# Weighted key-value recurrence on one core: logs, inverses and outputs in three successive slots, all even loads on GpSimd

## The chip, the cores and the metric

One core of a Trainium2 chip runs the program. The metric is the device time of the whole execution in microseconds. TensorE is PE, VectorE is DVE, ScalarE is ACT, GpSimd is POOL and SyncE is SP.

## The reference

For 16 sequences of 2048 steps and 256 channels, a decaying weighted mean of v with weights exp(k) is kept, in a form that is safe against overflow (pp is the running maximum):

```python
for t in range(seq_len):
    ww = u + kk
    qq = np.maximum(pp, ww)
    e1 = np.exp(pp - qq)
    e2 = np.exp(ww - qq)
    output[b, t, :] = (e1 * aa + e2 * vv) / (e1 * bb + e2 + 1e-08)
    ww = pp - w + kk
    qq = np.maximum(ww, kk)
    e1 = np.exp(ww - qq)
    e2 = np.exp(kk - qq)
    aa = e1 * aa + e2 * vv
    bb = e1 * bb + e2
    pp = qq
```

Here kk and vv are k and v at one time. aa, bb and pp are carried along the time, each with 256 channels, for each sequence by itself.

## The kernel before, in words

**Tiles.** Time lies on the partitions. The 2048 times are a head of 32 and 16 steps of TC = 126, each step two halves of 63. A pair is four sequences at one step: a tile `kr` and a tile `vr` of 126 x 4 x 256 numbers. So a step has four pairs, and with two pairs for the head there are NP = 66, numbered n. For each pair PE multiplies k by two triangular matrices (`logs`, L287, into `X`), ACT takes the exponential of the result (`exps`, L301 for the first eight pairs and L303 later, into `ez`), and DVE multiplies it by v (`times_v`, L319). `round_k` (L271, `km`) and `cast_v` (L311, `vb`) are DVE's casts ahead of these.

**State.** `sums` (L349) adds each half's totals of a step over the partitions into one bank, `tot`. After a step's last pair, at slot s, these totals are copied (`copy_sums`, L358), turned by PE (`turn_sums`, L365), split (`split_sums`, L372), and carried on by small DVE and ACT operations: a log (`lf`), offsets (`S`), a clamp (`near`), weights (`w`, `g`), the state itself (`tb`, `da`, `AB`), a log and an exponential for scaling (`y`, `phi`), a product (`ab`). PE turns the result (L455), DVE copies it to `row` (L460), and SyncE's transfers (L464, `inject`) write it as rows 126 and 127 of `ez` of the same step's pairs. With these rows in place the matmuls of `den` and `num` give the outputs of that step, the carried state included.

**Outputs.** Ten slots after its exponentials (six for the head) a pair's denominator is summed by PE (`den`, L488), ACT takes its log and exp(-log) (`recip`, L499 and L500), PE sums the numerator (`num`, L509, one half of the pair at a time), DVE multiplies (`mult`, L517) and the result is stored (`store`, L535).

**Slots and order.** The main loop's turn n is slot n. In it `exps(n)`, `recip(q)` for the pair q whose output is due, `num`, `mult` and `store` of the pair due one slot earlier, and `logs(n + 1)` are recorded; the order in which they are recorded is the order on each engine, since the helper `K` chains the instructions of an engine. After slot 65 only outputs are left. Small state operations stand at named places of the slot (`small_work`), by a table of slots after s.

**Buffers and banks.** Four `kr` and four `vr` tiles, so loads run four slots ahead; two `km` and two `vb`; seven `ez` tiles of two pairs each; five result tiles `rd`. Of the eight PSUM banks X takes four, den two (one tile), num one and tot one until slot 66; den's and num's tiles serve the two turns as well. After slot 65 den has two tiles and num three.

**Queues.** SP issues the v loads, the first k loads and the state rows; POOL issues the k loads (L128) and the stores. Both execute their lists in order.

Of the kernel before, what the change touches and what calls it, by code (L numbers as in the profile page):

```python
# [7 lines left out]
F32 = mybir.dt.float32  # L8
# [14 lines left out]
def kernel(  # L23
# [29 lines left out]
    TC = 2 * HS  # L53
# [54 lines left out]
    def load(n):  # L108
        kr = kpool.tile([128, 4, Dm], F32, tag="kr", name="kr")
        vr = vpool.tile([128, 4, Dm], F32, tag="vr", name="vr")  # L110
        kr_of[n], vr_of[n] = kr, vr
        c, p = pairs[n]
        if is_head(n):
            if p == 1:
                K(POOL.memset(kr[64:96, 0:2, :], 0.0))
                K(POOL.memset(vr[64:96, 0:2, :], 0.0))
            for t, x in ((kr, k), (vr, v)):
                for g in range(NG):
                    b = 6 * g + 4 * p
                    e = min(b + 2 * tiles_of(n), B)  # L120
                    if b < e:
                        K(SP.dma_start(out=t[g * GB:(g + 1) * GB, 0:e - b, :],
                                        in_=x[b:e, 0:T0, :].rearrange("n t d -> t n d")))
        else:
            t0 = T0 + c * TC
            r = min(128, T - t0)
            for t, x, eng in ((kr, k, SP if n <= AHEAD else POOL), (vr, v, SP)):
                K(eng.dma_start(  # L128
                    out=t[0:r, :, :], in_=x[4 * p:4 * p + 4, t0:t0 + r, :].rearrange("n t d -> t n d")))


# [252 lines left out]
        K(SC.activation(lf, st[c, "t"][:, 4:6], ACT.Ln))  # L384
        st[c, "lf"] = lf

    def state_offsets(c):
        lf = st.pop((c, "lf"))
        for h in range(2):
            i = 2 * c + h  # L390
            K(DVE.scalar_tensor_tensor(S[:, i + 1], S[:, i], 0.0, lf[:, h], ALU.max, ALU.add))
        near = tiny.tile([128, 3, 32], F32, tag="near", name="near")
        K(DVE.tensor_scalar(near, S[:, 2 * c:2 * c + 3], NEAR, -NEAR, ALU.min, ALU.max))
        st[c, "near"] = near
# [21 lines left out]
        K(DVE.scalar_tensor_tensor(AB[0][:, :, 0], by_two(st.pop((c, "g"))[:, 0]), 1.0, t[:, :, 0],  # L416
                                   ALU.min, ALU.mult))

    def state_step(c, h):
        if h == 0:  # L420
            t = st.pop((c, "t"))[:, 0:4].rearrange("p (q h) x -> p q h x", q=2)
            tb = small.tile([128, 2, 2, 32], F32, tag="tb", name="tb")
            K(DVE.scalar_tensor_tensor(tb, by_two(st.pop((c, "w"))), 1.0, t, ALU.min, ALU.mult))  # L423
            st[c, "tb"] = tb
        cur = AB[c]
        if h == 1:
            AB[c + 1] = small.tile([128, 2, 2, 32], F32, tag="AB", name="AB")
        da = tiny.tile([128, 2, 32], F32, tag=f"da{h}", name=f"da{h}")
        K(DVE.tensor_add(da, cur[:, :, h], st[c, "tb"][:, :, h]))
        K(DVE.scalar_tensor_tensor(cur[:, :, 1] if h == 0 else AB[c + 1][:, :, 0], by_two(st[c, "g"][:, h + 1]), 1.0,  # L430
                                   da, ALU.min, ALU.mult))

    def inject_logs(c):
        y = tiny.tile([128, 2, 32], F32, tag="y", name="y")
# [4 lines left out]
    def inject_weights(c):  # L439
        f = tiny.tile([128, 2, 32], F32, tag="phi", name="phi")  # L440
        K(SC.activation(f, st.pop((c, "y")), ACT.Exp, scale=-1.0, bias=cc[:, 5:6]))
        st[c, "phi"] = f

    def carries(c):

        ab = tiny.tile([128, 4, 2, 16], BF16, tag="ab16", name="ab16")
        f, f2 = st.pop((c, "phi")), tiny.tile([128, 2, 32], F32, tag="phi2", name="phi2")
        K(DVE.scalar_tensor_tensor(f2, st[c, "g"][:, 0:2], 1.0, f, ALU.max, ALU.min))
        K(DVE.tensor_mul(ab, AB[c].rearrange("p q h (j x) -> p (h j) q x", j=2),
                         f2.rearrange("p h (j x) -> p (h j) x", j=2).unsqueeze(2).broadcast_to([128, 4, 2, 16])))  # L450
        st[c, "ab"] = ab

    def turn_carries(c):
        d = bank("num", [128, D]) if wide else bank("den", [128, 2, D])[:, 0]
        K(PE.matmul(d[:, 0:128], st.pop((c, "ab")).rearrange("p m q x -> p (m q x)"), Id, start=True, stop=True))  # L455
        st[c, "d"] = d

    def inject(c):
        row = small.tile([128, 128], BF16, tag="row", name="row")
        K(DVE.tensor_copy(row, st.pop((c, "d"))[:, 0:128]))  # L460
        for j in range(2):
            for h in range(2):
                p = 64 * h + 32 * j
                K(SP.dma_start(out=EZ[group_of(c, j)][TC + h:TC + h + 1, 0:2, :, :].rearrange(  # L464
                                   "o q i (x c) -> o (q i x) c", c=128),
                               in_=row[p:p + 32, :]))

# [19 lines left out]
                            skip_group_check=True))  # L489
        DEN[n] = d  # L490

    def recip(n):
        r = NH if is_head(n) else TC
        i = tiles_of(n)
        rd = rpool.tile([128, 2, D], F32, tag="rd", name="rd")
        d = DEN.pop(n)
        for a in ((0, 1), (1, 2)) if n == NP - 1 else ((0, i),):
            a = slice(*a)
            K(SC.activation(rd[0:r, a, :], d[0:r, a, :], ACT.Ln, scale=RS))  # L499
            K(SC.activation(rd[0:r, a, :], rd[0:r, a, :], ACT.Exp, scale=-1.0))  # L500
        RD[n] = rd

    def num(n, i):
        if i >= tiles_of(n):
# [14 lines left out]
    def store(n):  # L519
# [10 lines left out]
        else:  # L530
            c, p = pairs[n]
            t0 = T0 + c * TC

            for a, b, eng in ((0, 2, POOL), (2, 4, SP)) if n == NP - 1 else ((0, 4, POOL),):
                K(eng.dma_start(out=out[4 * p + a:4 * p + b, t0:t0 + TC, :].rearrange("n t d -> t n d"),  # L535
                                in_=o[0:TC, a:b, :]))


    later = {}
    for c in range(-1, NST):  # L540
        s = last_of[c]
        work = [(s + 1, "sums", copy_sums), (s + 1, "last", turn_sums)]
        first, second = lambda c: state_step(c, 0), lambda c: state_step(c, 1)
        if c < 0:
            work += [(s + 2, "sums", split_sums), (s + 2, "act", state_logs),
                     (s + 3, "exp", state_weights), (s + 3, "pool", state_start)]
        else:
            work += [(s + 1, "last", split_sums), (s + 2, "first" if c else "exp", state_logs),
                     (s + 2, "sums", state_offsets), (s + 2, "sums", state_weights), (s + 2, "pool", first),
                     (s + 2, "act", inject_logs), (s + 3, "exp", inject_weights),  # L550
                     (s + 3, "pool", carries), (s + 3, "last", turn_carries), (s + 3, "last", inject)]
            if c + 1 < NST:
                work.append((s + 4 if c else s + 3, "pool", second))
            else:

                work = [(s + 1, "act", copy_sums), (s + 2, "sums", turn_sums), (s + 2, "sums", split_sums),
                        (s + 3, "first", state_logs), (s + 3, "sums", state_offsets), (s + 3, "act", state_weights),
                        (s + 3, "last", first), (s + 4, "act", inject_logs), (s + 4, "act", inject_weights),
                        (s + 4, "last", carries), (s + 5, "pool", turn_carries), (s + 5, "pool", inject)]
        for slot, where, f in work:  # L560
            later.setdefault((slot, where), []).append((f, c))

    def small_work(n, where):
        for f, c in later.pop((n, where), []):
            f(c)

    for slot, where, f in ((0, "exp", matrices_for_sums), (1, "pool", matrices_for_head),
                           (4, "dve", matrices_for_outputs),
                           (5, "dve", more_matrices_for_outputs)):
        later.setdefault((slot, where), []).append((lambda c, f=f: f(), None))  # L570

    patterns_for_head()
    round_k(0)
# [3 lines left out]
        K(DVE.tensor_copy(t[96:98], row_of(96, 98)))  # L577

    out_at = {n + (LAG - 4 if is_head(n) else LAG): n for n in range(NP)}
    for n in range(NP + LAG + 1):  # L580
        q, qp = out_at.get(n), out_at.get(n - 1)
        live, out_q, out_qp = n < NP, q is not None, qp is not None
        if n == NP:
            widen()
        if n + AHEAD < NP:
            load(n + AHEAD)
        small_work(n, "first")
        if live:
            exps(n)
        elif out_q:  # L590
            den(q)
            recip(q)
        small_work(n, "exp")
        if 0 < n <= NP:
            sums(n - 1)
        if n + 1 < NP:
            round_k(n + 1)
        small_work(n, "sums")
        if out_qp:
            num(qp, 0)  # L600
            if not live:
                num(qp, 1)
        if live and out_q:
            den(q)
            recip(q)
        if out_qp:
            mult(qp, 0)
            if live:
                num(qp, 1)
        small_work(n, "pool")  # L610
        if live:
            times_v(n)
        if out_qp:
            mult(qp, 1)
            store(qp)
        if n + 1 < NP:
            logs(n + 1)
            cast_v(n + 1)
        small_work(n, "dve")
        small_work(n, "act")  # L620
        small_work(n, "last")
    assert not later


# [28 lines left out]
```

## Time and profile before

| what | value |
|---|---|
| median of 5 runs | 334.43 us (330.21 to 335.71) |
| the profiled execution | 335.08 us, its span 333.4 us |
| busy: PE, DVE, ACT, POOL | 86%, 85%, 83%, 34% |
| granted TensorE clock, mean | 0.978 |
| HBM read and written | 68.10 MB and 33.55 MB, 305 GB/s over the span |
| DMA queue of POOL (q0) | 19232 packets, 65.27 MB |
| DMA queue of SP (q1) | 39858 packets, 36.93 MB |
| first and last start of L303 (pairs 8 to 65) | 39.5 and 290.9 us |

The page comes from one execution. A group of instructions has its source line, engine, output and input names, count, busy time, mean duration in ns, and the idle time just before it with what ended it. An arrow to the left reads "waited for". The DMA share is the mean busy share of sixteen DMA engines, summed over the queues.

### The profile page before, as it was taken

How to read it: one execution, taken by the hardware profiler on the slowest of the kernel's cores; microseconds unless marked ns; L12 is line 12 of the kernel's file. 1: busy time of each engine (PE TensorE's matmuls, PEld its weight loads, DVE VectorE, ACT ScalarE, POOL GpSimd, SP SyncE). 2: the span in 40 equal slices, each digit the busy share in tenths (PEclk: the TensorE clock that was granted, in tenths of full speed). 3: DMA queues.
4: the chain of work that ended last, by engine and by line, in shares of the span. 5: the costliest groups of instructions: out<-in, count | busy, mean ns of one | idle time of the engine just before them, and what ended most of it. 6: DMA issues, size and time to landing. Idle time of an engine off the chain costs nothing.

```text
span 333.4 us, 4078 instructions
## 1 busy us (share of the span) xinstructions
PE 286.9 (86%) x1200; PEld 137.3 (41%) x1200; DVE 284.3 (85%) x571; ACT 277.8 (83%) x310; POOL 114.3 (34%) x162
## 2 busy tenths in 40 slices
PE   0696988799999998999999999999998999998480
PEld 0333444344445453545454444444453545443130
DVE  2878798989898999999999989898989999968260
ACT  2647589699999999998999999999999998999370
POOL 6221224504243434425243434243334433122131
PEclk9999799999999999999999999999999999999787
DMA  7999859899999999999999999999999999747545
GB/s 250 240 336 340 285 176 329 248 310 331 326 376 348 374 343 375 328 366 342 377 329 373 349 373 342 346 361 343 373 353 369 311 304 316 237 130 214 161 147 164
DMA packets 59120, 102.47 MB, mean 307 GB/s; under 512 B 7610, under 2 KB 43162, under 8 KB 59098
## 3 DMA queue, kind: packets, MB, share of 16 engines
q0 software_dynamic: 19232, 65.27, 56.0%
q1 hardware_dynamic: 39858, 36.93, 36.3%
q8 instruction: 9, 0.15, 0.2%
q14 instruction: 13, 0.11, 0.1%
q10 hardware_dynamic: 8, 0.00, 0.0%
HBM read 68.10 MB, written 33.55 MB: 305 GB/s over the span
## 4 chain that ended last, share of the span: by engine, by line
PE 47%; DVE 26%; ACT 9%; DMA 7%; issue 7%; SPq 1%; POOL 0%; POOLq 0%; DVEq 0%; ACTq 0%
PE X L287 13%; PE num L509 12%; PE tot L349 11%; PE den L488 6%; DVE ez L319 6%; DVE rd L517 5%; DVE km L271 5%; DMA kr<-in_k_dram 5%; PE den L365 4%; ACT ez L303 4%; DVE vb L311 3%; DVE tsum L372 2%; DMA ez<-row 1%; DVE tb L423 1%; ACT rd L499 1%
## 5 line engine op out<-in xcount | busy, mean ns | idle before, releaser
L535 POOL DMA_DIRECT2D out_dram<-rd x64 | 58.6, 917 | 173.6 <-ACT rd L500 77.0
L303 ACT ACTIVATE ez<-X 128x2048 bf16<-128x2048 f32 x58 | 107.8, 1859 | 4.5 <-PE X L287 4.5
L517 DVE TENSOR_TENSOR rd<-num,rd 126x512 f32<-126x512 f32 (+1 forms) x131 | 88.8, 684 | 12.5 <-issue 7.1
L319 DVE TENSOR_TENSOR ez<-ez,vb 126x2048 bf16<-126x2048 bf16 (+1 forms) x66 | 79.8, 1209 | 2.6 <-ACT ez L301 2.1
L499 ACT ACTIVATE rd<-den 126x1024 f32<-126x1024 f32 (+2 forms) x67 | 67.0, 1000 | 12.3 <-PE den L488 11.7
L500 ACT ACTIVATE rd<-rd 126x1024 f32<-126x1024 f32 (+2 forms) x67 | 69.6, 1038 | 2.1
L287 PE MATMUL X<-km,NLE 128*128 128x512 f32 x128 | 52.7, 494 | 15.2 <-DVE km L271 12.8
L128 POOL DMA_DIRECT2D kr<-in_k_dram x61 | 48.0, 787 | 30.3 <-DVE km L271 11.6
L349 PE MATMUL tot<-ez,OHV 126*48 126x512 bf16 x128 | 50.1, 391 | 8.4 <-DVE ez L319 8.4
L509 PE MATMUL num<-ez,LfN 128*128 128x512 bf16 x128 | 49.8, 389 | 5.6 <-DVE rd L517 5.5
L349 PE MATMUL tot<-ez,OHE 128*48 128x512 bf16 x128 | 51.1, 399 | 0.0
L509 PE MATMUL num<-ez,IdN 126*128 126x512 bf16 (+1 forms) x131 | 50.5, 386 | 0.0
L271 DVE CAST km<-kr 126x1024 fp32r<-126x1024 f32 x64 | 44.6, 698 | 4.8 <-ACT km L205 4.7
L311 DVE CAST vb<-vr 126x1024 bf16<-126x1024 f32 (+1 forms) x66 | 45.2, 685 | 0.0
L488 PE MATMUL den<-ez,Lf 128*128 128x512 bf16 x128 | 39.0, 386 | 5.1 <-DMA ez<-row 4.5
L287 PE MATMUL X<-km,NLZ 128*128 128x512 f32 x128 | 41.1, 403 | 0.0
L488 PE MATMUL den<-ez,Id 126*128 126x512 bf16 (+1 forms) x131 | 40.0, 386 | 0.0
L287 PEld LDWEIGHTS X<-km,NLE 128*128 128x128 f32 x128 | 24.1, 196 | 27.7 <-DVE km L271 9.7
L287 PEld LDWEIGHTS X<-km,NLZ 128*128 128x128 f32 x128 | 24.8, 194 | 6.1 <-ACT ez L301 0.3
L349 PEld LDWEIGHTS <-OHE 128*48 128x48 bf16 x128 | 13.3, 104 | 33.5 <-issue 26.9
L509 PEld LDWEIGHTS <-LfN 128*128 128x128 bf16 x128 | 12.5, 98 | 32.4 <-issue 23.8
L509 PEld LDWEIGHTS <-IdN 126*128 126x128 bf16 (+1 forms) x131 | 12.9, 99 | 23.1 <-issue 21.6
(101 smaller groups left out, 204.9 us busy)
## 6 DMA issues: line engine op xcount, KB each, us to landing
out_dram<-rd POOLq DMA_DIRECT2D x63, 504.0 KB, 7.2
vr<-in_v_dram SPq DMA_DIRECT2D x60, 512.0 KB, 4.9
kr<-in_k_dram POOLq DMA_DIRECT2D x57, 512.0 KB, 8.2
vr<-in_v_dram SPq DMA_DIRECT2D x4, 504.0 KB
kr<-in_k_dram POOLq DMA_DIRECT2D x4, 504.0 KB, 10.7
kr<-in_k_dram SPq DMA_DIRECT2D x3, 512.0 KB, 6.4
ez<-row SPq DMA_DIRECT2D x64, 8.0 KB, 6.9
kr<-in_k_dram SPq DMA_DIRECT2D x3, 128.0 KB
```

The source lines that it names most:

```text
L271: K(DVE.tensor_copy(KM[n][0:r, 0:i, :], kr_of.pop(n)[0:r, 0:i, :]))
L287: K(PE.matmul(X[q][:, i, :], m[0:kr, :], km[0:kr, i, :], start=True, stop=True))
L303: K(SC.activation(ez_of(n)[:, 0:4:2], X[2][:, :, 0:i, :], ACT.Exp))
L311: K(DVE.tensor_copy(vb[0:r, 0:i, :], vr_of.pop(n)[0:r, 0:i, :]))
L319: K(DVE.tensor_mul(ez[0:r, 1:4:2], ez[0:r, 0:4:2], vb[0:r, 0:i, :].unsqueeze(1).broadcast_to([r, 2, i, D])))
L349: K(PE.matmul(TOT[c], m[0:r, :], ez_of(n)[0:r, q, i, :], start=n == first_of[c] and i == 0 and q == 0, stop=n == last_of[c] and i == tiles ...
L488: K(PE.matmul(d[:, i, :], m[0:r, :], ez_of(n)[0:r, q, i, :], start=q == 0, stop=q == 2, skip_group_check=True))
L499: K(SC.activation(rd[0:r, a, :], d[0:r, a, :], ACT.Ln, scale=RS))
L500: K(SC.activation(rd[0:r, a, :], rd[0:r, a, :], ACT.Exp, scale=-1.0))
L509: K(PE.matmul(d, m[0:r, :], ez_of(n)[0:r, q, i, :], start=q == 1, stop=q == 3, skip_group_check=True))
L517: K(DVE.tensor_mul(RD[n][0:r, i, :], NUM.pop((n, i))[0:r, :], RD[n][0:r, i, :]))
L535: K(eng.dma_start(out=out[4 * p + a:4 * p + b, t0:t0 + TC, :].rearrange("n t d -> t n d"), in_=o[0:TC, a:b, :]))
```

## The change

Outputs take three slots instead of two: `log_den` in slot n with `den`, `invert` in slot n + 1 ahead of the next pair's log, `num`, `mult` and `store` in slot n + 2. The loop has one slot more. Within a slot `logs(n + 1)` and `cast_v(n + 1)` now stand ahead of `times_v(n)`, and `sums(n)` follows in the same slot instead of the next. The state operations are single functions placed by plans for the head, the first step, the even steps and the last; in the even steps the state rows are issued in slot s + 5, for the first step in slot s + 4, for the last in s + 4.

From pair 4 on k and v are loaded by POOL (the two head pairs stay on SP). The 64 values of both halves go from `row` to `ez` in two transfers of 64 rows each instead of four of 32. A store is split: 120 partitions by POOL, the last six by SP; both halves of the last pair are split so.

Left out in the diff are the split of the state functions that only rearranges them, the old table of places, and the places of the constant matrices.

```diff
@@ -124,8 +124,8 @@
         else:
             t0 = T0 + c * TC
             r = min(128, T - t0)
-            for t, x, eng in ((kr, k, SP if n <= AHEAD else POOL), (vr, v, SP)):
-                K(eng.dma_start(
+            for t, x in ((kr, k), (vr, v)):
+                K((SP if n < 2 else POOL).dma_start(
                     out=t[0:r, :, :], in_=x[4 * p:4 * p + 4, t0:t0 + r, :].rearrange("n t d -> t n d")))
...
-    def state_offsets(c):
-        lf = st.pop((c, "lf"))
-        for h in range(2):
-            i = 2 * c + h
-            K(DVE.scalar_tensor_tensor(S[:, i + 1], S[:, i], 0.0, lf[:, h], ALU.max, ALU.add))
+    def state_offset(c, h):
+        i = 2 * c + h
+        K(DVE.scalar_tensor_tensor(S[:, i + 1], S[:, i], 0.0, st[c, "lf"][:, h], ALU.max, ALU.add))
+
+    def state_near(c):
         near = tiny.tile([128, 3, 32], F32, tag="near", name="near")
         K(DVE.tensor_scalar(near, S[:, 2 * c:2 * c + 3], NEAR, -NEAR, ALU.min, ALU.max))
         st[c, "near"] = near
...
+    def state_decay(c, h):
         if h == 1:
             AB[c + 1] = small.tile([128, 2, 2, 32], F32, tag="AB", name="AB")
-        da = tiny.tile([128, 2, 32], F32, tag=f"da{h}", name=f"da{h}")
-        K(DVE.tensor_add(da, cur[:, :, h], st[c, "tb"][:, :, h]))
-        K(DVE.scalar_tensor_tensor(cur[:, :, 1] if h == 0 else AB[c + 1][:, :, 0], by_two(st[c, "g"][:, h + 1]), 1.0,
-                                   da, ALU.min, ALU.mult))
+        K(DVE.scalar_tensor_tensor(AB[c][:, :, 1] if h == 0 else AB[c + 1][:, :, 0],
+                                   by_two(st[c, "g"][:, h + 1]), 1.0, st.pop((c, "da")), ALU.min, ALU.mult))
...
     def inject(c):
         row = small.tile([128, 128], BF16, tag="row", name="row")
         K(DVE.tensor_copy(row, st.pop((c, "d"))[:, 0:128]))
         for j in range(2):
-            for h in range(2):
-                p = 64 * h + 32 * j
-                K(SP.dma_start(out=EZ[group_of(c, j)][TC + h:TC + h + 1, 0:2, :, :].rearrange(
-                                   "o q i (x c) -> o (q i x) c", c=128),
-                               in_=row[p:p + 32, :]))
+            K(SP.dma_start(out=EZ[group_of(c, j)][TC:TC + 2, 0:2, :, :].rearrange(
+                               "h q i (x c) -> h (q i x) c", c=128),
+                           in_=row[64 * j:64 * j + 64, :]))
...
-    def recip(n):
+    def log_den(n, a=0, b=None):
         r = NH if is_head(n) else TC
-        i = tiles_of(n)
-        rd = rpool.tile([128, 2, D], F32, tag="rd", name="rd")
-        d = DEN.pop(n)
-        for a in ((0, 1), (1, 2)) if n == NP - 1 else ((0, i),):
-            a = slice(*a)
-            K(SC.activation(rd[0:r, a, :], d[0:r, a, :], ACT.Ln, scale=RS))
-            K(SC.activation(rd[0:r, a, :], rd[0:r, a, :], ACT.Exp, scale=-1.0))
-        RD[n] = rd
+        b = tiles_of(n) if b is None else b
+        if a == 0:
+            RD[n] = rpool.tile([128, 2, D], F32, tag="rd", name="rd")
+        K(SC.activation(RD[n][0:r, a:b, :], DEN[n][0:r, a:b, :], ACT.Ln, scale=RS))
+
+    def invert(n, a=0, b=None):
+        r = NH if is_head(n) else TC
+        b = tiles_of(n) if b is None else b
+        K(SC.activation(RD[n][0:r, a:b, :], RD[n][0:r, a:b, :], ACT.Exp, scale=-1.0))
...
-            for a, b, eng in ((0, 2, POOL), (2, 4, SP)) if n == NP - 1 else ((0, 4, POOL),):
-                K(eng.dma_start(out=out[4 * p + a:4 * p + b, t0:t0 + TC, :].rearrange("n t d -> t n d"),
-                                in_=o[0:TC, a:b, :]))
+            for a, b in ((0, 2), (2, 4)) if n == NP - 1 else ((0, 4),):
+                for r0, r1, eng in ((0, 120, POOL), (120, TC, SP)):
+                    K(eng.dma_start(
+                        out=out[4 * p + a:4 * p + b, t0 + r0:t0 + r1, :].rearrange("n t d -> t n d"),
+                        in_=o[r0:r1, a:b, :]))
...
+    PLANS = {
+        "head": ((1, "a0", copy_sums), (1, "p1", turn_sums), (1, "d5", split_sums), (2, "a1", state_logs),
+                 (3, "a0", state_weights), (3, "d4", state_start)),
+        "first": ((1, "a0", copy_sums), (1, "p1", turn_sums), (1, "d5", split_sums), (2, "a0", state_logs),
+                  (2, "d4", state_offset, 0), (2, "d4", state_offset, 1), (2, "d4", state_near),
+                  (2, "a1", state_weights), (3, "d0", state_sums), (3, "d0", state_add, 0),
+                  (3, "d1", state_decay, 0), (3, "a0", inject_logs), (3, "a1", inject_weights),
+                  (4, "d0", carry_weights), (4, "d0", carries), (4, "p0", turn_carries), (4, "d1", inject),
+                  (4, "d4", state_add, 1), (4, "d5", state_decay, 1)),
+        "steady": ((1, "a0", copy_sums), (1, "p1", turn_sums), (1, "d5", split_sums), (2, "a0", state_logs),
+                   (2, "d4", state_offset, 0), (2, "d5", state_offset, 1), (3, "d0", state_near),
+                   (3, "a0", state_weights), (3, "d4", state_sums), (3, "d5", state_add, 0),
+                   (4, "d0", state_decay, 0), (4, "a0", inject_logs), (4, "a0", inject_weights),
+                   (4, "d5", carry_weights), (5, "d0", carries), (5, "p0", turn_carries), (5, "d1", inject),
+                   (5, "d4", state_add, 1), (5, "d5", state_decay, 1)),
+        "last": ((1, "a0", copy_sums), (1, "p1", turn_sums), (1, "d5", split_sums), (2, "a0", state_logs),
+                 (2, "d2", state_offset, 0), (2, "d2", state_offset, 1), (2, "d2", state_near),
+                 (2, "a1", state_weights), (3, "d0", state_sums), (3, "d0", state_add, 0),
+                 (3, "d0", state_decay, 0), (3, "a1", inject_logs), (3, "a1", inject_weights),
+                 (4, "d0", carry_weights), (4, "d0", carries), (4, "p0", turn_carries), (4, "d1", inject)),
+    }
...
+        for slot, where, f, *args in PLANS["head" if c < 0 else "first" if c == 0 else
+                                           "last" if c + 1 == NST else "steady"]:
+            at(last_of[c] + slot, where, f, c, *args)
...
     out_at = {n + (LAG - 4 if is_head(n) else LAG): n for n in range(NP)}
-    for n in range(NP + LAG + 1):
-        q, qp = out_at.get(n), out_at.get(n - 1)
-        live, out_q, out_qp = n < NP, q is not None, qp is not None
+    for n in range(NP + LAG + 2):
+
+        q, qi, qp = out_at.get(n), out_at.get(n - 1), out_at.get(n - 2)
+        live, more, out_q, out_qi, out_qp = n < NP, n + 1 < NP, q is not None, qi is not None, qp is not None
         if n == NP:
             widen()
         if n + AHEAD < NP:
             load(n + AHEAD)
-        small_work(n, "first")
         if live:
             exps(n)
-        elif out_q:
-            den(q)
-            recip(q)
-        small_work(n, "exp")
-        if 0 < n <= NP:
-            sums(n - 1)
-        if n + 1 < NP:
+        small_work(n, "d0")
+        if more:
             round_k(n + 1)
-        small_work(n, "sums")
         if out_qp:
             num(qp, 0)
             if not live:
                 num(qp, 1)
-        if live and out_q:
+        small_work(n, "p0")
+        small_work(n, "d1")
+        small_work(n, "a0")
+        if out_qi and qi < NP - 1:
+            invert(qi)
+        if out_q:
             den(q)
-            recip(q)
+            if q < NP - 1:
+                log_den(q)
+            else:
+                for i in range(2):
+                    log_den(q, i, i + 1)
+                    invert(q, i, i + 1)
         if out_qp:
             mult(qp, 0)
             if live:
                 num(qp, 1)
-        small_work(n, "pool")
+        small_work(n, "d2")
+        if more:
+            cast_v(n + 1)
+        small_work(n, "d3")
+        if more:
+            logs(n + 1)
         if live:
             times_v(n)
+        small_work(n, "p1")
+        if live:
+            sums(n)
+        small_work(n, "d4")
         if out_qp:
             mult(qp, 1)
             store(qp)
-        if n + 1 < NP:
-            logs(n + 1)
-            cast_v(n + 1)
-        small_work(n, "dve")
-        small_work(n, "act")
-        small_work(n, "last")
+        small_work(n, "d5")
+        small_work(n, "a1")
     assert not later
 
```

## The prediction, made before the changed kernel was run

> **What bounds the kernel now.** I read the page's busy shares first, then the windows, the waits of the even stretch, the timeline of one step, and last the end of the run. Four pairs of images make one time step; slot n is one turn of the main loop.
>
> ```profile
> PE 286.9 (86%) x1200; PEld 137.3 (41%) x1200; DVE 284.3 (85%) x571; ACT 277.8 (83%) x310; POOL 114.3 (34%) x162
> ...
> L303 ACT ACTIVATE ez<-X 128x2048 bf16<-128x2048 f32 x58 | 107.8, 1859 | 4.5 <-PE X L287 4.5
> L517 DVE TENSOR_TENSOR rd<-num,rd 126x512 f32<-126x512 f32 (+1 forms) x131 | 88.8, 684 | 12.5 <-issue 7.1
> L319 DVE TENSOR_TENSOR ez<-ez,vb 126x2048 bf16<-126x2048 bf16 (+1 forms) x66 | 79.8, 1209 | 2.6 <-ACT ez L301 2.1
> L499 ACT ACTIVATE rd<-den 126x1024 f32<-126x1024 f32 (+2 forms) x67 | 67.0, 1000 | 12.3 <-PE den L488 11.7
> L500 ACT ACTIVATE rd<-rd 126x1024 f32<-126x1024 f32 (+2 forms) x67 | 69.6, 1038 | 2.1
> ```
>
> Three engines are equally full. The windows show that the even stretch is fuller still, and the end is not:
>
> ```profile
> 200.00:220.00 20.00, 19.07 (x84) 9.45 (x83) 19.01 (x37) 18.80 (x21) 7.28 (x9) 1.00 1.03 346
> 310.00:320.00 10.00, 7.04 (x19) 2.56 (x20) 2.20 (x4) 3.77 (x4) 1.59 (x2) 0.66 0.41 123
> ```
>
> Columns are PE, PEld, DVE, ACT, POOL busy, clock, DMA share, GB/s. At 95% on three engines no single one is the limit: they wait for each other. The waits between 100 and 280 us, ten steps:
>
> ```profile
> ACT lf L384 <- DVE tsum L372: 6.8, 10, 0.7
> PE tot L349 <- DVE ez L319: 5.6, 10, 0.6
> DVE tb L423 <- ACT w L403: 3.8, 10, 0.4
> PE num L509 <- DVE rd L517: 3.5, 20, 0.2
> ACT rd L499 <- PE den L488: 3.4, 10, 0.6
> ```
>
> Each is a state operation, or a log, standing one slot too close to what it needs; no load is waited for. The big exponentials time the slots:
>
> ```profile
> 60.77 1.88 ACT L303 ACTIVATE ez<-X 128x2048 bf16<-128x2048 f32 x1 [1.74 <-PE X L287]
> ...
> 290.88 1.86 ACT L303 ACTIVATE ez<-X 128x2048 bf16<-128x2048 f32 x1
> ```
>
> These are pairs 13 and 65: 230.1 us / 52 = 4.425 us a slot, 17.70 a step. At the end:
>
> ```profile
> 307.28 3.74 SPq L464 DMA_DIRECT2D ez<-row  x4
> 312.96 1.01 PE L488 MATMUL den<-ez,Lf 128*128 128x512 bf16 x2 [4.48 <-DMA ez<-row]
> 314.87 1.02 ACT L499 ACTIVATE rd<-den 126x1024 f32<-126x1024 f32 x1 [5.03 <-PE den L488]
> ```
>
> The last step's state rows cost a stop of 4.5 us, after which PE runs at half rate (den's second pair begins 0.81 us after the first instead of 0.43) until 319.
>
> **The Trainium skill.** DMA: Bandwidth & Descriptors, "Why a DMA increments its semaphore by 16 and not by 1": a SyncE transfer uses the largest number of engines up to 16 that divides the slowest dimension of both sides. By this the old row transfers (32 rows on both sides) used 16 engines, the new (destination 2 x 32 x 128) use 2; no run here shows it yet. Same page, "SWDGE vs HWDGE vs iDMA": the DMA engine alternates between queues at packet boundaries. The trace agrees on packet size: q0 carries 65.27 MB in 19232 packets, q1 36.93 in 39858. SBUF — State Buffer, "Who interferes with whom": two-port copies on VectorE can lock GpSimd out of writing descriptors; here a load's issue takes 0.77 us beside a busy VectorE, which includes it.
>
> **The even stretch, step by step.** Start-to-start times from the timeline around 150 us. ACT: exponential 1.75 (152.75 to 154.50), inverse 0.97; log 1.05 if its inverse follows, estimated 0.92 if not. DVE: cast or product 0.60, product with v 1.13. PE: first num 0.44, den 0.88, second num to X 0.25, X 1.21, sums 0.99: 3.77 a slot, and 1.02 + 0.16 a step for the two turns: 16.26. Small ACT and DVE operations as their rows say, less 0.08 overlap. A crossing to another engine costs 0.05.
>
> Now each slot's PE order is num, den, num, X, sums; ACT exponential, inverse of the slot before, log; DVE km, product, vb, product with v, product. Plain slot: num0 ends 0.60, product 0.65 to 1.33, second num 1.38, X 1.63 to 2.91, product with v 1.85 to 3.07, sums' second matmul 3.12, slot ends 3.87. ACT has 0.2 to spare. With the state work (s is a step's last slot):
> - s+1 = s+5: state product and km on DVE, then the row copy ends at 1.04 and den starts at 1.09 instead of 0.44; X 2.22; the turn of the sums waits for the log, which now stands behind copy and inverse and ends at 3.31: no wait, 3.35 to 4.38; sums end at 5.37.
> - s+2: offsets go after the product with v, hidden: 3.87.
> - s+3: clamp before km moves the product to 0.92, X to 1.90, sums' second matmul to 3.39: 4.14.
> - s+4: state decay before km does nearly the same: 4.11.
>
> Together 17.49 against 17.70. From pair 13 to 65 are 13 steps: **-2.7 us**. A later log and an earlier cast thus save what ACT waited for den and den's bank, and leave PE and DVE in one loop (product with v, sums, num0, product, vb), whose round is the 3.87. My pieces are good to about 0.3 a step, 4 us in all.
>
> **Transfers.** Per slot GpSimd issues two loads and a store: 2 x 0.77 + 0.92 = 2.5 of 4.4 us, hidden behind its waits for the products (173.6 us idle before stores). In its order loads stand behind the store that waits for the second product, as k did before. The built order has each GpSimd transfer wait for the eighth before it, 2.7 slots or 11.6 us, against landings of 7 to 8.5 now. A result buffer is held one slot longer: log to landed store some 9 us plus 2 slots' work against five slots; free about 2 us early. All this costs nothing while loads land in the 11 us they have. v leaves 1 KB packets; six rows of a store on SyncE, 24 KB, are small.
>
> State rows: 1.9 us to landing for the transfers at 44.6 us on a quiet machine, with two rows an engine. 30 more rows each take q1's mean packet (1109 us / 22883 = 48 ns), and at worst one q0 packet between (1849 us / 12208 = 151 ns): 3.3 us at least, 7.9 at most if no backlog is added. I take 7.9 when the queue is full and 5.5 when half full. They are issued at 1.09 in slot s+5 and wanted at 0.44 in slot s+7: 5.37 + 3.87 + 0.44 - 1.09 = 8.6 us. So hidden, by 0.7. In the first step only one slot lies between (about 3.7 us): 5.5 - 3.7 = **+1.8**.
>
> **The end**, counted from E, the end of the last big exponential (292.74 before, with 40.66 us to the span's end). Copy of sums at E+2.5, turned and split by 4.63, log 4.87, offsets to 5.8, exponents 7.33, state to 8.1, phi 9.7, row 10.9: issue at 11.0, where before it was 14.5. But the rows of the step before now leave only at E+3.9, land at 9.4, and its den, wanted at 7.1 for a log at 8.2, holds ACT for 2.3 us. So the last rows land at 11.0 + 2.3 + 5.5 = 18.8 and the log after them starts at about 20. From there 3 x 2.02 + 2.39 us to the last inverse (as 318.28 on shows), then 8.8 instead of 8.57 to the end, the last half now being the second issue on GpSimd: E+36.9 to 37.2. **-3.5 to -3.8**; I take -3.8 with the extra 0.3 beside it. If rows land in 3.3 us it is -7, if in 8, +1.5.
>
> Sum: -2.7 + 1.8 - 3.8 + 0.3 = -4.4 on the profiled 335.08 (span 333.4 and 1.7 around it): 330.7. That execution is 0.65 above the median, so **330.0**, 1.3% faster.
>
> **Rivals.**
> - One ring is the bound. q0 moved 41.66 MB between 100 and 280 us in 64.2% of the time: 360 GB/s when full. A step is 4 x 1528 KiB = 6.26 MB, 17.4 us on a full ring; at 97% full 17.9, +0.2 a step instead of -0.2: -4.4 + 5.3 gives 335. For: share 1.03 in the windows. Against: it is the sum over two queues, slices reach 390 GB/s, and no load is waited for.
> - Slower: the rows on two engines land late. Before, two rows an engine took 7.2 us median, 11.1 at most, behind v. From 8.6 us on, each us is a wait of den in every step, with num, X and so all engines behind it in PE's order. At 9.6: +13 for 13 steps, the end only -1, the start +3: -2.7 + 13 - 1 + 3 + 0.3 = +12.6, 347. Against: v is gone from that queue.
> - The rows land in about 3.3 us: start 0, end -7: -2.7 - 7 + 0.3 = -9.4, 325.
> - The separation doesn't help: if the turn of the sums waits 0.3 longer for the later log, the step is 17.8 and the gain is the end's alone: 334.
>
> **Chances.** Forecast 0.40, fast rows 0.12, full ring 0.16, no gain of the separation 0.10, late rows 0.22. About 1% can be told from no change. The forecast's own range is 326 to 334. Faster takes 0.33 of the forecast and all fast rows: 0.45. Slower takes the late rows and a third of the ring and the separation: 0.31. Same: 0.24. The range 323 to 345 leaves out the late rows beyond some 9.5 us, about half of that case, and the far edge of the fast rows.
>
> **What would show it.** Right: no more L499 behind den in the even stretch, slots of 3.9 to 4.1 and one of 5.4, rows issued some 13 us after E, den after it waiting under 2 us. Wrong: den waiting for ez<-row in every step (late rows), km or vb waiting for loads (ring), a turn of sums waiting for the log.

## The result, and the profile after: the time is longer, and den waits for the state rows

The changed kernel has a median of 342.84 us (334.74 to 352.84) against 333.24 us (330.21 to 340.54) for the kernel before. The ratio is 1.0123, with a 95% interval of 1.0078 to 1.0168. Like every ratio below, it counts only fast executions, those within 1.5% of the fastest of the same kernel (four of the changed kernel's), so it lies below the ratio of the medians, 1.029. The profiled executions are 345.88 us long with a span of 344.1, against 335.08 and 333.4.

The page of the kernel after (busy share and count; queues with packets, MB and share; groups with busy time, mean ns, then idle time before them and its main cause):

```profile
PE 286.2 (83%) x1200; PEld 136.8 (40%) x1200; DVE 284.1 (83%) x571; ACT 274.4 (80%) x310; POOL 168.7 (49%) x226
...
q0 software_dynamic: 27424, 96.95, 86.6%
q1 hardware_dynamic: 7334, 5.25, 5.8%
...
L493 PE MATMUL den<-ez,Lf 128*128 128x512 bf16 x128 | 39.0, 386 | 18.6 <-DMA ez<-row 11.1
```

PE and DVE have as much work as before; the span only holds more idle time. The windows show where (PE, PEld, DVE, ACT, POOL busy, clock, DMA share, GB/s):

```profile
200.00:220.00 20.00, 17.01 (x76) 8.18 (x75) 17.46 (x34) 16.81 (x19) 10.04 (x12) 1.00 1.02 357
325.00:335.00 10.00, 8.84 (x39) 3.58 (x37) 6.85 (x11) 9.78 (x13) 3.89 (x5) 1.00 0.90 272
```

In the even stretch PE, DVE and ACT fall from about 19 to about 17 of 20 us. The second window lies 17 to 27 us after the end of the last big exponential, as 310 to 320 us did before; it is fuller, PE 8.8 instead of 7.0 us and ACT 9.8 instead of 3.8. den is now L493, the log L502, the rows' transfers L469, the stores L542. The waits between 100 and 280 us name the idle time (us in total, times, longest):

```profile
ACT rd L502 <- PE den L493: 11.4, 14, 1.9
PEld L493 <- DMA ez<-row: 9.6, 6, 2.4
...
PE den L493 <- DMA ez<-row: 5.1, 4, 1.9
```

Before, no den of this stretch waited for rows. One step in the timelines of SyncE, PE and ACT:

```profile
122.57 1.15 SPq L469 DMA_DIRECT2D ez<-row  x2
...
132.71 0.60 PE L493 MATMUL den<-ez,Lf 128*128 128x512 bf16 x2 [1.27 <-DMA ez<-row]
...
139.14 1.02 ACT L502 ACTIVATE rd<-den 126x1024 f32<-126x1024 f32 x1 [0.66 <-DMA out_dram<-rd]
```

The rows take 132.71 - 122.57 = 10.1 us to arrive, and PE stands for the last 1.3. A little later the log waits for a second transfer, a store that holds its result tile. Seven of the 13 steps from pair 13 to 65 waited for rows, and the same reading gives 9.8 to 10.8 us in them; in the other six den came 9.3 to 11.5 us after the issue and found the rows there. The big exponentials at pairs 13 and 65:

```profile
63.15 1.88 ACT L303 ACTIVATE ez<-X 128x2048 bf16<-128x2048 f32 x1 [1.09 <-PE X L287]
...
305.93 1.88 ACT L303 ACTIVATE ez<-X 128x2048 bf16<-128x2048 f32 x1
```

242.78 us for 13 steps is 18.68 a step, where it was 17.70: +12.7 us. (In nearly every kernel the first of these 13 steps is 1 us or more shorter than the others; the mean is over all.) The start costs 63.15 - 60.77 = +2.4. From the end of the last big exponential to the end of the span there are 36.3 us instead of 40.66: -4.4. The three make +10.7, the difference of the spans.

### The profile page after: what moved, and what is told of

The parts are those of the page before. It is cut to its first block, busy times and chain, and to the rows that moved or that the text cites. A ratio compares the mean times of both kernels' runs of the same rounds, so it can differ in the third digit from the quotient of the medians.

```text
span 344.1 us, 4145 instructions
## 1 busy us (share of the span) xinstructions
PE 286.2 (83%) x1200; PEld 136.8 (40%) x1200; DVE 284.1 (83%) x571; ACT 274.4 (80%) x310; POOL 168.7 (49%) x226
## 4 chain that ended last, share of the span: by engine, by line
PE 29%; DMA 28%; DVE 20%; ACT 12%; issue 7%; ACTq 0%; POOL 0%; POOLq 0%; DVEq 0%; SPq 0%
DMA out_dram<-rd 16%; DMA ez<-row 11%; PE tot L349 7%; PE num L515 7%; PE X L287 6%; PE den L493 6%; DVE ez L319 6%; DVE rd L523 5%; ACT rd L502 4%; DVE vb L311 3%; PE den L365 3%; DVE km L271 3%; ACT rd L507 3%; ACT ez L303 2%; ACT ez L301 2%
## 5 line engine op out<-in xcount | busy, mean ns | idle before, releaser
L542 POOL DMA_DIRECT2D out_dram<-rd x65 | 53.1, 817 | 136.4 <-issue 77.7
L303 ACT ACTIVATE ez<-X 128x2048 bf16<-128x2048 f32 x58 | 108.7, 1875 | 13.5 <-PE X L287 12.9
L502 ACT ACTIVATE rd<-den 126x1024 f32<-126x1024 f32 (+2 forms) x67 | 66.9, 998 | 26.9 <-PE den L493 21.9
L287 PE MATMUL X<-km,NLE 128*128 128x512 f32 x128 | 53.0, 496 | 14.6 <-DVE km L271 12.6
L128 POOL DMA_DIRECT2D kr<-in_k_dram x62 | 53.8, 867 | 21.0 <-DVE km L271 13.4
L128 POOL DMA_DIRECT2D vr<-in_v_dram x62 | 54.8, 884 | 0.1
L493 PE MATMUL den<-ez,Lf 128*128 128x512 bf16 x128 | 39.0, 386 | 18.6 <-DMA ez<-row 11.1
L349 PE MATMUL tot<-ez,OHV 126*48 126x512 bf16 x128 | 49.2, 385 | 1.4 <-DVE ez L319 1.1
L311 DVE CAST vb<-vr 126x1024 bf16<-126x1024 f32 (+1 forms) x66 | 48.4, 733 | 0.0
L493 PE MATMUL den<-ez,Id 126*128 126x512 bf16 (+1 forms) x131 | 39.6, 382 | 0.0
L493 PEld LDWEIGHTS <-Lf 128*128 128x128 bf16 x128 | 11.8, 99 | 36.4 <-DMA ez<-row 17.1
## 6 DMA issues: line engine op xcount, KB each, us to landing
vr<-in_v_dram POOLq DMA_DIRECT2D x4, 504.0 KB, 11.6
```

Of the source, the lines that this page charges most:

```text
L128: K((SP if n < 2 else POOL).dma_start(out=t[0:r, :, :], in_=x[4 * p:4 * p + 4, t0:t0 + r, :].rearrange("n t d -> t n d")))
L287: K(PE.matmul(X[q][:, i, :], m[0:kr, :], km[0:kr, i, :], start=True, stop=True))
L303: K(SC.activation(ez_of(n)[:, 0:4:2], X[2][:, :, 0:i, :], ACT.Exp))
L311: K(DVE.tensor_copy(vb[0:r, 0:i, :], vr_of.pop(n)[0:r, 0:i, :]))
L349: K(PE.matmul(TOT[c], m[0:r, :], ez_of(n)[0:r, q, i, :], start=n == first_of[c] and i == 0 and q == 0, stop=n == last_of[c] and i == tiles ...
L493: K(PE.matmul(d[:, i, :], m[0:r, :], ez_of(n)[0:r, q, i, :], start=q == 0, stop=q == 2, skip_group_check=True))
```

## The experiments

Each was compared with runs of the kernel before on its own chip. A step is the mean from pair 13 to 65 in the profile of that run; "after" is the changed kernel. The landing of rows is the time from their issue to their arrival, the room the time from their issue to the den that needs them.

| run | median, us | ratio, 95% interval | step, us |
|---|---|---|---|
| after | 342.84 | 1.0123 (1.0078 to 1.0168) | 18.68 |
| a_rows4 | 332.7 | 0.9996 (0.9958 to 1.0035) | 17.83 |
| a_vsp | 352.35 | 1.05 (1.0421 to 1.058) | 19.60 |
| a_vsp_rows4 | 349.04 | 1.0175 (1.01 to 1.025) | 17.95 |
| b_pool | 332.73 | 1.0 (0.9973 to 1.0026) | 17.72 |
| a_rows4_two_eng | 341.83 | 1.0245 (1.0182 to 1.0308) | 18.60 |
| a_first_plan | 346.11 | 1.0366 (1.0302 to 1.0431) | 18.57 |
| b_rows2 | 336.48 | 1.0007 (0.9965 to 1.0049) | 18.15 |
| a_rows4_last120 | 335.06 | 1.0059 (1.0029 to 1.0089) | 17.71 |
| a_store1 | 344.5 | 1.0276 (1.0199 to 1.0352) | 18.41 |
| a_rows4_late | 411.97 | 1.2315 (1.2219 to 1.241) | 23.43 |
| a_rows4_halfstore | 326.47 | 0.9834 (0.9777 to 0.989) | 17.50 |
| a_rows4_vlast | 340.77 | 1.0245 (1.0183 to 1.0307) | 18.06 |
| b_end_general | 334.5 | 1.0038 (1.0009 to 1.0067) | 17.82 |
| b_end_slot | 329.4 | 0.9882 (0.982 to 0.9944) | 17.76 |

### Rows or ring: a_rows4, b_pool

a_rows4 puts the old form of the rows' transfers into after:

```diff
-            K(SP.dma_start(out=EZ[group_of(c, j)][TC:TC + 2, 0:2, :, :]...,
-                           in_=row[64 * j:64 * j + 64, :]))
+            for h in range(2):
+                p = 64 * j + 32 * h
+                K(SP.dma_start(out=EZ[group_of(c, j)][TC + h:TC + h + 1, 0:2, :, :]...,
+                               in_=row[p:p + 32, :]))
```

> The changed kernel with the state rows in four transfers of 32 rows, as before; all else as changed. Theory A (late rows: two transfers of 64 rows land late because each runs on few DMA engines): den no longer waits for ez<-row in the even stretch, a step takes about 17.5 us, the start loses the 2.8 us wait, and the time is 329 to 332 us. Theory B (full ring: all large transfers stand in POOL's one queue, which the 96% share shows full, and rows and stores land late only because of that): the step stays above 18.2 us, waits for results' stores take the place of those for rows, and the time is 337 to 343 us.

b_pool is before with k and v of all pairs from pair 4 on loaded by GpSimd, as in after.

> The kernel before with k and v of all pairs from 2 on loaded by POOL (the head pairs stay on SP), nothing else. Theory A: the rows have four slots there, so 332 to 334 us, no change. Theory B: POOL's queue is as full as in the changed kernel, steps lengthen to 18 us or more, 337 us or more.

From the timelines of a_rows4, and GpSimd's queue in b_pool between 100 and 280 us:

```profile
118.85 3.78 SPq L471 DMA_DIRECT2D ez<-row  x4
...
127.57 0.60 PE L495 MATMUL den<-ez,Lf 128*128 128x512 bf16 x2
```

```profile
q0 software_dynamic: 17987, 62.48, 100.0%
```

a_rows4 is rid of the whole slowdown, with all loads still on GpSimd. Its den starts 8.7 to 9.0 us after the rows' issue; in one of the 13 steps it waited for them, and started after 10.0. b_pool fills the same ring (GpSimd's DMA queue) and is as fast as before. So moving the loads is not what costs; the form of the rows' transfers is, in the room that the new plan leaves.

### v beside the rows: a_vsp, a_vsp_rows4

```diff
-                K((SP if n < 2 else POOL).dma_start(
+                K((SP if n < 2 or x is v else POOL).dma_start(
```

> The changed kernel with the v loads on SP, as before; rows still in two transfers. Theory A: the rows now stand behind v in SP's queue and land later still, den waits for them in every step, 345 us or more. Theory B: POOL's queue falls from 96% to about 64% share, the step falls to 17.5 to 17.8 us and the time to 329 to 334 us.

> The changed kernel with both: v loads on SP and the rows in four transfers. What is left is the order of the slots and the split store. Theory A and theory B agree that it is about 326 to 331 us if the separation of logs and inverses gains what the prediction's step sum says (17.5 us a step, a shorter end); 333 or more if the separation itself costs.

Two 64-row transfers behind v took up to 13.8 us from issue to den, four of 32 up to 11.7, with waits of den of up to 2.8 us in the even stretch of a_vsp_rows4. No theory had foreseen that the four also come late. The kernel before bears such rows, since its den comes 13.5 us after their issue. So v in front of the rows does cost, where den wants them after 8.7 us, and the move of v to GpSimd is needed by the new plan.

### Number of transfers or number of engines: a_rows4_two_eng

Four transfers of 32 rows as in a_rows4, but cut the other way, 16 rows for each of two partitions (the product `ab` is laid out in the order that this needs, not shown):

```diff
+            for q in range(2):
+                p = 64 * j + 32 * q
+                K(SP.dma_start(out=EZ[group_of(c, j)][TC:TC + 2, q:q + 1, :, :]...,
+                               in_=row[p:p + 32, :]))
```

> The kernel after with the state rows in four transfers of 32 rows, as in a_rows4, but each transfer holds 16 rows of each of the two destination partitions (destination 2 x 16 x 128 instead of 1 x 32 x 128). Engines (A): by the divisor rule each transfer still has only two DMA engines; whatever the number and size of the transfers, 64 packets a half stand on two engines, the landing stays about 10 us against the 8.6 us of slack, den waits for ez<-row in most steps of the even stretch, mean step 18.5 to 18.8, 338 to 343 us. Size (B): if it is the 64-row length of one transfer that makes it late, four short ones land as in a_rows4 and the time is 332 to 335 us, without a wait of den.

The time is that of the engine theory: with count and length as in a_rows4, the spread alone costs some 9 us. The place of the wait is not the one expected: den waited for rows once in the even stretch, 1.0 us, and in six of the 13 steps started 8.7 to 9.0 us after their issue without a wait, so the rows did not take the 10 us expected of them there. ACT's log waits for result tiles instead. From the waits between 100 and 280 us:

```profile
ACT rd L504 <- DMA out_dram<-rd: 8.5, 3, 3.4
```

From the timelines of SyncE and ACT:

```profile
154.30 2.72 SPq L471 DMA_DIRECT2D ez<-row  x4
157.62 13.27 SPq L544 DMA_DIRECT2D out_dram<-rd  x4
...
172.07 1.02 ACT L504 ACTIVATE rd<-den 126x1024 f32<-126x1024 f32 x1 [3.08 <-DMA out_dram<-rd]
```

There are five result tiles, so this log needs the tile stored three slots earlier. SyncE issued the six rows of that store at 157.62 (the first of the four in this line), just behind the state rows; 172.07 is 14.4 us later. The other 120 rows of it, twenty times the bytes, landed 9.7 us after their issue on GpSimd. The Trainium skill (DMA: Bandwidth & Descriptors, "Why a DMA increments its semaphore by 16 and not by 1") says that SyncE's transfers take the lowest-numbered of the engines, as many as the divisor rule gives: two for such rows, six for the six-row stores. Rows on two engines and the six-row stores then share those two, and what is queued behind the rows comes late with them. The runs agree with it; no view shows single engines.

### The stores or the rows: a_store1

```diff
-                for r0, r1, eng in ((0, 120, POOL), (120, TC, SP)):
+                for r0, r1, eng in ((0, TC, POOL),):
```

> The kernel after with each store as one transfer of 126 rows on GpSimd; SyncE carries only the two 64-row transfers. Queue (A): the rows by themselves still land in about 10 us, den's waits for ez<-row stay (28 us in the whole profile of after, less in better runs), and only the waits of the log for a result buffer go, which come from the six-row stores standing behind the rows on the same DMA engines (4.5 us in after, 8.5 us in a_rows4_two_eng): 337 to 341 us. Rival (B): the six-row stores ahead of the rows make the rows late: without them the rows land inside 8.6 us, no wait of den, 331 to 334 us. If the six-row stores do nothing: 341 to 344 us.

The waits of the log for a result tile are gone, and den's stay: in five steps it starts 10.1 to 12.5 us after the issue. The waits between 63 and 280 us:

```profile
PEld L493 <- DMA ez<-row: 8.4, 5, 2.4
...
PE den L493 <- DMA ez<-row: 5.9, 4, 1.9
```

So the two transfers of 64 rows are late by themselves, with nothing else of size on SyncE's queue. The time is no better than that of after; the estimate of 337 to 341 was too low.

### More room for the same rows: a_first_plan, b_rows2

```diff
-        for slot, where, f, *args in PLANS["head" if c < 0 else "first" if c == 0 else
+        for slot, where, f, *args in PLANS["head" if c < 0 else "first" if c + 1 < NST else
```

> The kernel after, its two 64-row transfers unchanged, but every step except the last follows the plan of the first step, which issues the rows one slot earlier (slot s+4 instead of s+5). Slack (A): the slack of the rows grows from 8.6 to about 12.5 us, the rows still take about 10 us to land, and den no longer waits for them in the even stretch; what the tighter plan costs on the other engines stays: 333 to 337 us. If the two-engine rows do harm in another way than by their late landing (B, for instance by delaying the loads and stores that share the two engines), the steps stay at 18.5 us or more and the time at 340 to 344 us.

b_rows2 is before with its rows in two transfers of 64.

> The kernel before with the state rows in two 64-row transfers instead of four of 32, nothing else changed. Slack (A): its rows leave two to three slots earlier in the even stretch, so some 10 us of landing, perhaps 12 behind v on the same queue, stay hidden: step 17.7 as before; only the end, where den waits for the last rows, is longer by 0 to 3 us: 332.5 to 336 us, ratio 1.00 to 1.01. If two engines do harm in another way than by the row's landing (B): a ratio of 1.02 or more.

Both have den 13.5 us after the issue. a_first_plan's list of waits holds no ez<-row in the even stretch, as expected. Its time was missed all the same: from pair 21 on every step but the last is 18.72 us, one slot of the four 6.2. From the waits between 100 and 280 us:

```profile
ACT w L403 <- DVE near L393: 11.9, 10, 1.2
```

Its clamp is made just ahead of the weights that need it, in every step, so I put the longer step down to the plan; the same plan with four transfers, which would show it, was not run. By this reading the looser plan of after is worth about 1.1 us a step (18.72 against the 17.5 to 17.8 of a_rows4), if its rows arrive.

b_rows2 keeps before's steps of 17.77 us up to pair 49. Later its rows outlast even the room of before once:

```profile
255.47 1.16 SPq L462 DMA_DIRECT2D ez<-row  x2
...
271.61 0.61 PE L486 MATMUL den<-ez,Lf 128*128 128x512 bf16 x2 [2.44 <-DMA ez<-row]
```

That is 16.1 us, with v on the same queue. The ratio is 1.0007, but the median is 3.5 us above that of before, so it is not shown that the new form costs nothing where there is room.

### What the landing costs on sixteen engines: a_rows4_late

```diff
-                   (4, "d5", carry_weights), (5, "d0", carries), (5, "p0", turn_carries), (5, "d1", inject),
-                   (5, "d4", state_add, 1), (5, "d5", state_decay, 1)),
+                   (4, "d5", carry_weights), (5, "d4", state_add, 1), (5, "d5", state_decay, 1),
+                   (6, "d0", carries), (6, "p0", turn_carries), (6, "d1", inject)),
```

> a_rows4 with carries, turn_carries and inject of the even stretch one slot later (s+6 instead of s+5): this measures the landing of the four 32-row transfers beside a full GpSimd ring, which a_rows4 hides. The rows then have some 3.5 to 4 us before den wants them. The prediction's estimates for rows: 3.3 at least, 7.9 at most. If the four transfers land in about 7 us, as in the kernel before (7.2 median): a wait of den of 2.5 to 4 us in every step, mean step 20.0 to 21.5, 362 to 382 us less what the other engines catch up, so 355 to 380. If they land in about 3.3 to 4 us, the steps stay near 17.9 and the time near 333 to 336.

```profile
123.85 3.85 SPq L471 DMA_DIRECT2D ez<-row  x4
...
132.25 1.01 PE L495 MATMUL den<-ez,Lf 128*128 128x512 bf16 x2 [4.46 <-DMA ez<-row]
```

8.4 us here, 7.7 to 8.9 over all twelve steps, although the ring is no longer full (83% between 100 and 280 us). The old form too needs most of the 8.7 us that the new plan leaves. The step is 1.9 us longer than the worst estimate: more is lost than the wait. After it den takes 1.01 us instead of 0.60 (the granted clock of this run is 0.894 in the mean, that of a_rows4 0.985), and what else follows was not taken apart.

### Where the gain went: a_rows4_halfstore, a_rows4_last120, a_rows4_vlast

With the rows in time a_rows4 should have won the forecast's 4.4 us and won nothing. a_rows4_halfstore leaves half of each pair's output unwritten, except for the last pair:

> a_rows4 with only the first two of four images of each pair stored (all but the last pair); the products are computed as before, and half of the output is left unwritten. DMA bytes of a step fall from 6.26 to 5.23 MB, a sixth less. If the DMA engines (98 per cent busy in a_rows4) are what keeps the steps at 17.54 and 17.85 and makes the last loads late (12 us instead of 8.5): steps 17.4 to 17.5, no wait for loads or result buffers at the end, 327 to 330 us. If it is the engines' own order of work: 331 to 333 us, as a_rows4.

```profile
61.17 1.88 ACT L303 ACTIVATE ez<-X 128x2048 bf16<-128x2048 f32 x1 [1.39 <-PE X L287]
...
288.72 1.88 ACT L303 ACTIVATE ez<-X 128x2048 bf16<-128x2048 f32 x1
```

227.55 / 13 = 17.50 us a step against 17.83: the engines can do the step that the prediction worked out, and the DMA traffic takes the difference. (No log of a_rows4 waits for a result tile, so it is not that these come free sooner.) It doesn't take it evenly. In a_rows4 the steps alternate between 17.5 and 17.8; one is 18.65, with the one wait for rows, and the last is 20.28 where a_rows4_halfstore has 17.55. That last step alone is 2.7 of the 4.2 us. Its loads are late, as DVE's timeline and the landings of what was issued between 260 and 290 us show (KB each, median us to landing). DVE waits 1.14 us for a k and 0.48 for a v there; the rest of the 2.7 was not taken apart.

```profile
288.75 0.69 DVE L271 CAST km<-kr 126x1024 fp32r<-126x1024 f32 x1 [1.14 <-DMA kr<-in_k_dram]
```

```profile
out_dram<-rd POOLq DMA_DIRECT2D x7, 480.0 KB, 10.5
kr<-in_k_dram POOLq DMA_DIRECT2D x4, 504.0 KB, 11.9
vr<-in_v_dram POOLq DMA_DIRECT2D x4, 504.0 KB, 12.7
```

Two attempts on that did not help: a_rows4_last120 splits the last four pairs' loads into 120 and 6 rows, and a_rows4_vlast has their v on SyncE.

> a_rows4 (four 32-row transfers) with the loads of the last step, which hold 126 rows, split as the stores are: 120 rows on GpSimd and 6 on SyncE. Theory: in a_rows4 the loads and stores near 260 to 290 us landed late (10 to 14 us instead of 7 to 8)[...]; with 120 and 6 rows they land as the others do, the last step's slots of 5 to 6 us fall to 4.0 to 4.9, about 3 us are saved: 329 to 331 us, ratio 0.985 to 0.995. Rival: the ring is simply full (98 per cent between 100 and 280 us), and the last loads are late because the rings are behind by then: no change, 332 to 334 us.

> a_rows4 with v of the last step's four pairs on SyncE, all other loads on GpSimd: two queues share the last loads and stores. If the order within GpSimd's one queue makes the last loads and stores late: they land 2 to 4 us earlier, 329 to 331 us. If the DMA engines as a whole are behind by then (98 per cent busy): no change, 332 to 334 us; rows of the step before may then be late behind v, up to +3 us.

With 120 rows the last loads land in 11.6 and 12.6 us, and the last step still takes 19.4: six rows less do not help. In a_rows4_halfstore too, with a sixth fewer bytes, the last k loads take 8.5 us where the others take 7.0. With the last v on SyncE, k still takes 11.1, and one den waits 5.3 us for rows issued in the midst of these v loads. Why the last loads take longer than the 8.5 and 9.0 us of the others stays open.

### The end by itself: b_end_general, b_end_slot

Before, with the last step's state work earlier and nothing else changed. b_end_general deletes the last step's own table of places; b_end_slot moves it by one slot:

```diff
-                        (s + 3, "first", state_logs), (s + 3, "sums", state_offsets), (s + 3, "act", state_weights),
-                        (s + 3, "last", first), (s + 4, "act", inject_logs), (s + 4, "act", inject_weights),
-                        (s + 4, "last", carries), (s + 5, "pool", turn_carries), (s + 5, "pool", inject)]
+                        (s + 2, "pool", state_logs), (s + 2, "last", state_offsets), (s + 2, "last", state_weights),
+                        (s + 3, "sums", first), (s + 3, "act", inject_logs), (s + 3, "act", inject_weights),
+                        (s + 3, "last", carries), (s + 4, "pool", turn_carries), (s + 4, "pool", inject)]
```

> The kernel before with the last step's state work on the plan of the other steps, so that its rows leave two slots earlier (slot s+3 instead of s+5); nothing else changed. If the end's gain is a thing of its own (the prediction's step of -3.8, of which a_rows4 showed -3.4 in its profile): the 4.5 us stop of den for the last rows shrinks or goes, 328.5 to 331 us, ratio 0.985 to 0.995. Rival: the state work now stands ahead of the tail's own den, log and products on ACT and DVE, and the rows still meet the stores on the DMA engines: the stop is paid elsewhere, 332 to 334 us.

> The kernel before with the last step's state work moved one slot earlier instead of two (logs after the first product of slot s+2, rows in s+4). If the end's gain is a thing of its own: half to all of the 4.5 us stop goes, 329.5 to 331.5 us. Rival as for b_end_general: 332 to 334 us.

In b_end_general the turn of the carries stands in PE's order before ACT and DVE have its product, and the old stop comes back there; the last step up to pair 65 also takes 19.3 us, with one v load awaited for 1.85:

```profile
308.09 0.23 PE L455 MATMUL num<-Id,ab 128*128 128x128 bf16 x1 [3.76 <-DVE ab L449]
```

In b_end_slot it waits 1.18 us, as before, and den waits only 0.27 us for the rows:

```profile
305.47 2.68 SPq L464 DMA_DIRECT2D ez<-row  x4
...
308.67 0.59 PE L488 MATMUL den<-ez,Lf 128*128 128x512 bf16 x2 [0.27 <-DMA ez<-row]
```

From the last big exponential's end to the span's end it takes 328.0 - 292.28 = 35.7 us instead of 40.66. This kernel, before with three lines of its table changed, is the fastest that computes everything: 329.4 us, 1.2% under before.

## Why the prediction was wrong, by its own steps

- **The state rows: the step that failed.** "3.3 us at least, 7.9 at most if no backlog is added. I take 7.9 when the queue is full ... So hidden, by 0.7." The room was right: 8.6 worked out, 8.7 to 9.0 seen in a_rows4. The landing was 9.8 to 10.8 in the seven steps that waited. The sum began from 1.9 us, read on a quiet machine; beside a full ring even the old form takes 7.7 to 8.9 (a_rows4_late), so the backlog that was set aside is most of it. The extra for two engines was put at up to 6 us and is about 2, by these two runs. Two errors that ran against each other left 2.5 us, and the margin was 0.7.
- **The evidence was at hand and was argued away.** The late-rows rival quoted 7.2 us median for the old rows and set against it that v had left their queue. b_pool has no v there either, and its rows took 7.0 us median. v lengthens some landings (a_vsp_rows4), not the usual one.
- **The late-rows rival** gave +12.6 us on the profile at a landing of 9.6; the profile shows +10.7 at about 10.4. Its mechanism is what happened, though not every step waits: after a stop the next rows often are in time, and steps of 17.4 to 17.5 and 19.5 to 20.0 us alternate, counted from pair 14.
- **The even stretch, -2.7.** The engines' sum was right in its total: 17.49 predicted, 17.50 in a_rows4_halfstore. That they meet so well is partly luck: 17.49 was worked out for an even step, but 17.50 and before's 17.70 are means that hold the short first step. Without it a_rows4_halfstore has 17.59 and before 17.78. The gain isn't reached in after because of the rows, nor in a_rows4, where the DMA engines leave a mean of 17.83. The ring rival had put that at 17.9 and 335 us, and a_rows4 measured 332.7: even with the rows in time the forecast would have missed this gain. The rival had a longer step everywhere; most of the loss came in the last step. "No load is waited for", held against it, was read off a kernel whose loads were on two queues.
- **Transfers.** "Six rows of a store on SyncE, 24 KB, are small" counted bytes. Behind the rows they held a result tile that was thought free 2 us early (waits of 2.7 us in sum between 100 and 280 us).
- **The start,** +1.8 predicted, +2.4 measured: 5.9 us of landing instead of 5.5. With four transfers it is +0.2.
- **The end,** -3.5 to -3.8 predicted, -4.4 in after, -3.4 in a_rows4. In after the last rows leave at 320.28, 12.5 us after the last big exponential's end (13.3 predicted), and no den waits for them. b_end_slot, -4.9 alone, shows that it needed nothing of the rest.

What is not settled: the runs of after range from 334.74 to 352.84 us. A landing that hovers about the room it has would do that, but no run isolates it.

## What to carry to other kernels

Take the landing of a small transfer from the traffic that it will meet, not from a quiet stretch, before shortening the room that hides it; with 0.7 us of margin on 8 count on a wait. Two transfers fewer are no saving if the outer dimension of those left shrinks to two: ask how each form is spread over the DMA engines, and what is queued behind it. And try the parts of a bundle singly: here the last step's state work, one slot earlier on the kernel before, gave more than the whole.

## What the runs showed of the hardware that was not expected

- The same 32 KB of rows in four transfers: cut as 1 x 32 x 128 the kernel takes 332.7 us, cut as 2 x 16 x 128 it takes 341.83.
- A 24 KB store on SyncE took 14.4 us behind such rows, while its 480 KB part on GpSimd took 9.7.
- Four row transfers land in 7.7 to 8.9 us beside a busy ring, but den had its rows 3.2 us after the issue near the end, where only stores are left (b_end_slot).
- Loads of 120 partitions landed no sooner than loads of 126 (11.6 and 11.9 us for k).
